# Sparse attention over 128 rows with zero-padded keys, dilated attention with its input in residue order

## The chip, the cores and the metric

One NeuronCore of a Trainium2 chip runs the whole program in one launch. The metric is device microseconds of that core. Five engines matter: TensorE (PE, with its weight loads shown apart as PEld), VectorE (DVE), ScalarE (ACT), GpSimd (POOL), and SyncE (SP), which issues the transfers. Every engine works through its own instructions in order.

## What is computed

The reference is two transformer blocks on 512 tokens of width 1024. The first mixes three branches (a gated linear recurrence, sparse attention, gated linear attention) and ends in a dense feed-forward. The second is a state-space mixer and a dilated-attention mixer, each followed by a mixture of 32 experts. The change touches the sparse attention of the first block and the dilated attention of the second.

```python
# sparse attention: 16 heads in 4 groups g of 4 heads r, head dim 64
kc = compress_blocks(k_cmp, ...)          # 31 compressed keys per group
o_cmp = softmax(q . kc + bias) . vc
sel   = top 8 of 8 blocks of 64 keys      # all blocks, 512 tokens
o_slc = softmax(q . k_slc + bias) . v_slc # causal
o_win = softmax(q . k_win + bias) . v_win # last 256 keys
o = g0 * o_cmp + g1 * o_slc + g2 * o_win
# dilated attention: groups (window, dilation) = (128,1), (512,4), (2048,16)
q, k = rope(x @ wq), rope(x @ wk);  v = x @ wv
o, m, l = attention of each residue class of tokens mod dilation
```

## The kernel before, in words

Large products are split into a high part in fp32r and a low remainder, three matmuls for each 128-deep slice: high x high, high x low, low x high. `piece2` loads 256 weight columns (1 MB) into one of the weight slots (`wslot` goes round a list, `self.order`, of five), ACT makes the high part `whi`, DVE and POOL the remainders. `g_fm2` (matmul on L351) then writes features by tokens with 512 token columns moving, two blocks of 128 features each of 24 matmuls; `g_tm2` (L368) writes tokens by features with 256 columns moving, four blocks of 24 matmuls.

**Sparse attention.** `cmp_keys` puts the keys and values to be compressed into `kt`, `cmp_hidden` multiplies them by `cmp_w1` (L659, plain fp32, 155 columns gathered from `kt` with a step of 16 elements), `cmp_out` forms the compressed keys `kcH`, `kcL` and values `vc`. For each group `nsa_q` makes the queries `Q`: 64 rows hold the high part and the other 64 rows the low part, so one 128-row matmul against the high keys, copied into both halves (`KH`, L827), adds both. The low keys `KL` have 64 rows that hold data; a second matmul (L828) takes only these 64 rows of `Q` and of `KL`. So 128-row and 64-row matmuls alternate:

```python
nc.tensor.matmul(w, lhsT=Q[:, i, qs], rhs=KH[:, ty, k0:k1], start=True, ...)
nc.tensor.matmul(w, lhsT=Q[H, i, qs], rhs=KL[H, ty, k0:k1], stop=True, ...)
```

`nsa_cmp` does the same with 32 compressed keys (L782 with `kcH`, L784 with `kcL`). `nsa_a` adds the bias and takes maximum, exponential and scale on DVE, ACT and POOL; `nsa_c` transposes the weights (L851, four heads a time), splits them (`ph` on ACT, `pl` on DVE) and multiplies with `V` (L855, L856). The compressed part of it has 32 rows: four transposes of 128x32, then two 512-column matmuls with 32 rows against `vc`.

`nsa` walks over 32 steps, one for a group, a block of 128 queries and a kind (selected, window). While step n is in its `nsa_c`, step n+1 is in its `nsa_a`, and units of projections that come later (`Fill`) are put between. The order on each engine is then made by the framework's planner.

**Dilated attention.** `att_begin` and `att_tile` transpose the layer-normed input, 128 tokens a time, in the tail of the first expert stage (`transpose_split`, L433 and L434), tokens in their natural order. `att_qk` projects queries and keys by `g_fm2`, turns them by rope, and POOL writes the sum in residue order: for the 16-fold and 4-fold groups at once, for the queries of group 0 in four pieces. `att_v` projects values of the groups 1 and 2 by `g_tm2` with every fourth token column of `xT` as the weights that are loaded (`tok=lambda v, t: v[:, t::4]`), so each block of 128 tokens is one residue class, and ACT copies it out. `att` then runs the three groups with `att_a` (scores L1758, softmax) and `att_c` (L1784 transposes, L1793 products), projections of the next group between them as fill: `att_v(2)` beside group 0, `att_v(1)` beside the first half of group 1.

Of the kernel before, what the change touches and what calls it, by code (L numbers as in the profile page):

```python
# [88 lines left out]
def make_consts():  # L89
# [16 lines left out]
    c.add("am0", np.where(np.concatenate([k >= tq, k <= tq], 1), 0.0, BIG))  # L106
# [44 lines left out]
class Base:  # L151
# [206 lines left out]
    def g_tm2(self, segs, x, evac, tok=lambda v, t: v[:, 128 * t:128 * t + 128]):  # L358
# [4 lines left out]
        for t in range(4):  # L363
            ps = self.mm("lin", "lin")
            for k in range(8):
                xh, xl = x(k)
                for i, (w, v) in enumerate(((hi, xh), (lo, xh), (hi, xl))):
                    nc.tensor.matmul(ps[:, :width], lhsT=tok(v, t), rhs=w[:, k, :width],  # L368
                                     start=(k == 0 and i == 0), stop=(k == 7 and i == 2))
                if self.fine and k == 3:  # L370
                    yield
# [52 lines left out]
    def transpose_split(self, src, hi, lo, t):  # L424
# [3 lines left out]
        for h in range(2):  # L428
# [4 lines left out]
            nc.scalar.activation(hi[:, 4 * h:4 * h + 4, c], v, AF.Copy)  # L433
            nc.vector.tensor_tensor(lo[:, 4 * h:4 * h + 4, c], v, hi[:, 4 * h:4 * h + 4, c], op=OP.subtract)  # L434


class Block1:
# [144 lines left out]
    def nsa_tables(self, st, q):  # L582
# [5 lines left out]
        self.vc = p.tile([32, 4, 128], R, name="vc")  # L588
# [33 lines left out]
    def cmp_setup(self, st):  # L622
        q = self.cq = self.pool(st, "cmp", side="right")

        self.ckt = [q.tile([128, 5, 512], F, name=f"kt{i}") for i in range(2)]
        pos = q.tile([32, 2, 64], F, name="pos")
        self.nc.sync.dma_start(pos, self.a["cmp_pos"][0].rearrange("y j d -> j y d"))
        for ty in range(2):
# [4 lines left out]
            pv = pp[:64, :32].rearrange("p (j e) -> p e j", e=2)  # L633
            for e in range(2):
                self.nc.vector.tensor_copy(t[64 * e:64 * e + 64, 4, 0:32:2], pv[:, e])

    def cmp_keys(self, x):

        nc = self.nc
        for ty in range(2):  # L640
            def ev(j, ps):
                t = self.ckt[ty]
                for h in range(2):
                    s = ps[64 * h:64 * h + 64]
                    nc.scalar.activation(t[0:64, 2 * j + h], s, AF.Copy)
                    nc.vector.tensor_copy(t[64:128, 2 * j + h, 0:511], s[:, 1:512])
# [3 lines left out]
    def cmp_hidden(self, ty):  # L650
# [5 lines left out]
        for m in range(2):  # L656
            ph = self.mm("ph", "lg")
            for j in range(16):
                nc.tensor.matmul(ph[:, 0:155], lhsT=w1[j // 8][:, j % 8, 128 * m:128 * m + 128],  # L659
                                 rhs=self.ckt[ty][:, :, 2 * j:2 * j + 481:16], start=(j == 0), stop=(j == 15))  # L660
# [16 lines left out]
    def cmp_out(self, ty):  # L677
# [3 lines left out]
        if ty == 0:  # L681
# [5 lines left out]
            nc.vector.tensor_copy(z[:, :, 0:31], pk[:64, :124].rearrange("p (g c) -> p g c", g=4))  # L687
            for e in range(2):
                r = slice(64 * e, 64 * e + 64)
                nc.scalar.activation(self.kcH[r], z, AF.Copy)  # L690
                nc.vector.tensor_tensor(self.kcL[r], z, self.kcH[0:64], op=OP.subtract)
        else:
# [11 lines left out]
            nc.scalar.activation(self.vc[:, :, 0:64], zh, AF.Copy)  # L704
            nc.vector.tensor_copy(self.vc[:, :, 64:128], zl)
# [17 lines left out]
    def nsa_kv(self, hf, x):  # L723
        nc, w_in, p = self.nc, self.a["w_in"][0], self.ngp
        o = hf * 128
        KL = p.tile([128, 2, 512], R, name="KL", bufs=2)
        for g in range(2):
            self.nK[2 * hf + g] = p.tile([128, 2, 512], R, name="KH", bufs=3), KL
            self.nV[2 * hf + g] = p.tile([128, 4, 2, 128], R, name="V", bufs=3)

        def ev_k(j, ps):
            for g in range(2):
                s = ps[64 * g:64 * g + 64]
                KH = self.nK[2 * hf + g][0]
# [38 lines left out]
    def nsa_cmp(self, g):  # L773
# [3 lines left out]
        H = slice(64 * (g % 2), 64 * (g % 2) + 64)  # L777
        pc = self.mm("pc", "lg")
        pcv = pc.rearrange("p (b h c) -> p b h c", b=4, h=4)
        for b in range(4):  # L780
            for h in range(4):
                nc.tensor.matmul(pcv[:, b, h], lhsT=Q[:, h, 128 * b:128 * b + 128], rhs=self.kcH[:, g],  # L782
                                 start=True, stop=False, skip_group_check=True)
                nc.tensor.matmul(pcv[:, b, h], lhsT=Q[H, h, 128 * b:128 * b + 128], rhs=self.kcL[H, g],  # L784
# [18 lines left out]
    def nsa_a(self, g, b, ty, out):  # L803
# [3 lines left out]
        H = slice(64 * (g % 2), 64 * (g % 2) + 64)  # L807
# [11 lines left out]
        for h in range(4):  # L819
            at = h % per * n  # L820
            if at == 0:
                ps = self.mm("lg", "lg")
                buf = sp.tile([128, 512], F, name="S", bufs=8)
                for i in range(h, h + per):
                    for c, k0, k1 in rng:
                        w = ps[:, (i - h) * n + c:(i - h) * n + c + k1 - k0]
                        nc.tensor.matmul(w, lhsT=Q[:, i, qs], rhs=KH[:, ty, k0:k1], start=True, stop=False, skip_group_check=True)  # L827
                        nc.tensor.matmul(w, lhsT=Q[H, i, qs], rhs=KL[H, ty, k0:k1], start=False, stop=True, skip_group_check=True)  # L828
# [17 lines left out]
    def nsa_pv(self, O, src, V, first, last, n=128):  # L846
# [3 lines left out]
        for h in range(4):  # L850
            nc.tensor.transpose(pt[:n, 128 * h:128 * h + 128], src(h), self.ident)  # L851
        ph = tp.tile([128, 512], R, name="ph")[:n]
        pl = tp.tile([128, 512], R, name="pl")[:n]
        self.split(pt[:n], ph, pl)
        nc.tensor.matmul(O, lhsT=V, rhs=ph, start=first, stop=False, skip_group_check=True)  # L855
        nc.tensor.matmul(O, lhsT=V, rhs=pl, start=False, stop=last, skip_group_check=True)  # L856

    def nsa_c(self, g, b, ty, A, C, yd):
# [11 lines left out]
        for i, (pos, kb) in enumerate(order):  # L870
            self.nsa_pv(O, lambda h: S[h][:, 128 * pos:128 * pos + 128], V[:, kb, ty], ty == 0 and i == 0, False)
# [1486 lines left out]
```

## Time and profile before

| | us |
|---|---|
| three runs | 3441.3, 3443.03, 3443.37 |
| median | 3443.03 |
| the profiled execution, its own time | 3444.63 |
| span of its profile (first to last instruction) | 3442.8 |
| PE busy | 3286.1 (95%) |
| DVE, ACT, POOL busy | 1474.6, 1008.2, 731.6 |

The span is cut into stretches by the program's order: setup and recurrence up to about 170 us, compression of keys and first projections up to about 280 us, sparse attention 280 to 632 us, then gated linear attention, merge, feed-forward, state-space mixer, the first experts (from about 1928 us), dilated attention 2516 to 2832 us, and the second experts up to the end. An engine counts as busy from the start of an instruction to its modelled end, so PE reads full even where its matmuls follow one another slowly; the distance between the starts of two matmuls tells how fast it goes.

### The profile page before, as it was taken

Reading aid. Unit: us, or ns where it says so; the run is one execution under the profiler, and the core shown is the slowest. Engines: PE = TensorE matmul, PEld = TensorE weight load, DVE = VectorE, ACT = ScalarE, POOL = GpSimd, SP = SyncE. Lnnn points to the kernel's source line nnn. Section 1 sums busy time; section 2 is a strip of 40 time slices with the busy share of each in tenths; the row PEclk is TensorE's granted clock in tenths of the full one; section 3 lists DMA queues with packets and bytes.
Section 4 is the critical chain, followed back from the end, with each engine's and each line's share of the span. In section 5 each row is a group of like instructions: output and inputs, shape, how many; then the busy total and the mean of one; then the engine's idle time right before and its main releaser. Section 6 shows DMA issues by size and latency. Waiting matters only on the chain. (4 is left out here: it accounts for less than half of the span.)

```text
span 3442.8 us, 40245 instructions
## 1 busy us (share of the span) xinstructions
PE 3286.1 (95%) x15295; PEld 2263.3 (66%) x15295; DVE 1474.6 (43%) x3023; ACT 1008.2 (29%) x1871; POOL 731.6 (21%) x567
## 2 busy tenths in 40 slices
PE   6899999999998999999999899999999988999997
PEld 5677777787886888877777544444489885444443
DVE  4835455632224323278777522222453445222223
ACT  3525444742233222244333201000233332000001
POOL 2422222432333222103333200000163412000000
PEclk9999897999998999999999899999999998999999
DMA  8231111123333233233332699999821225999996
GB/s 186 86 115 46 42 37 31 50 86 116 117 117 119 90 95 98 63 110 99 106 107 96 249 389 362 380 351 351 308 62 50 62 86 214 390 360 378 356 347 254
DMA packets 289986, 599.26 MB, mean 174 GB/s; under 512 B 29104, under 2 KB 150316, under 8 KB 289756
## 3 DMA queue, kind: packets, MB, share of 16 engines
q1 hardware_dynamic: 289788, 596.63, 50.0%
q8 instruction: 123, 2.02, 0.2%
q14 instruction: 75, 0.61, 0.1%
HBM read 584.94 MB, written 11.60 MB: 173 GB/s over the span
## 5 line engine op out<-in xcount | busy, mean ns | idle before, releaser
L332 POOL TENSOR_TENSOR lob<-rawb,whi 128x1024 fp32r<-128x1024 f32 (+1 forms) x53 | 137.0, 2586 | 791.0 <-ACTq L2156 538.4
L262 PE MATMUL mm<-hT,whi 128*128 128x512 f32 x960 | 300.0, 394 | 0.0
L351 PE MATMUL lin<-hT,whi 128*128 128x512 f32 (+1 forms) x784 | 268.5, 421 | 21.7 <-ACT gs L534 15.9
L2076 PE MATMUL mm<-rawb,XG 128*64 128x512 f32 x704 | 262.1, 600 | 0.0
L2076 PE MATMUL mm<-rawa,XG 128*64 128x512 f32 x704 | 258.4, 599 | 0.0
L242 DVE TENSOR_TENSOR loa<-rawa,whi 128x1024 fp32r<-128x1024 f32 (+2 forms) x94 | 116.8, 1243 | 298.4 <-ACT whi L241 297.0
L242 POOL TENSOR_TENSOR lob<-rawb,whi 128x1024 fp32r<-128x1024 f32 x56 | 141.7, 2530 | 438.8 <-ACT whi L241 395.9
L262 PEld LDWEIGHTS mm<-hT,whi 128*128 128x128 f32 x960 | 180.7, 188 | 44.1 <-ACT hT L433 0.2
L241 ACT ACTIVATE whi<-rawa 128x1024 fp32r<-128x1024 f32 (+2 forms) x94 | 94.6, 1006 | 357.6 <-issue 191.8
L351 PEld LDWEIGHTS lin<-hT,whi 128*128 128x128 f32 (+1 forms) x784 | 152.2, 197 | 65.5 <-ACT gs L534 16.8
L2211 PEld LDWEIGHTS xg<-OH,X 128*128 128x128 f32 x1024 | 133.3, 195 | 78.1 <-issue 74.6
L2139 PE MATMUL cmb<-yy,sel 128*128 128x512 f32 x512 | 156.3, 428 | 13.1 <-ACT yy L2119 3.6
L2139 PEld LDWEIGHTS cmb<-yy,sel 128*128 128x128 f32 x512 | 90.7, 192 | 112.4 <-issue 59.5
L2211 PE MATMUL xg<-OH,X 128*128 128x256 f32 x1024 | 153.5, 298 | 2.7 <-DVE OH L2201 2.7
L389 POOL TENSOR_TENSOR ln<-lnv,mhalf 128x1 f32<-128x1 f32 x16 | 13.4, 840 | 605.7 <-DVE lnv L387 602.1
L368 PE MATMUL lin<-whi,hT 128*128 128x256 f32 x640 | 130.1, 294 | 0.8 <-ACT gv L952 0.8
L262 PE MATMUL mm<-xT,whi 128*128 128x512 f32 (+1 forms) x400 | 129.5, 404 | 1.2 <-ACT xT L433 1.2
L2113 PE MATMUL py<-rawa,H 128*64 128x512 f32 x288 | 129.9, 598 | 0.0
L2076 PEld LDWEIGHTS mm<-rawa,XG 128*64 128x64 f32 x704 | 69.9, 136 | 89.9 <-issue 83.6
L2113 PE MATMUL py<-rawb,H 128*64 128x512 f32 x288 | 126.6, 598 | 0.0
L351 PE MATMUL lin<-xT,whi 128*128 128x512 f32 x384 | 123.5, 399 | 0.0
L2076 PE MATMUL mm<-mraw,XG 128*64 128x512 f32 x336 | 123.3, 602 | 0.0
(609 smaller groups left out, 7355.3 us busy)
## 6 DMA issues: line engine op xcount, KB each, us to landing
rawa<-in_moe_w_up_dram SPq DMA_DIRECT2D x92, 512.0 KB, 7.7
rawb<-in_moe_w_up_dram SPq DMA_DIRECT2D x92, 512.0 KB, 10.2
rawa<-in_moe_w_gate_dram SPq DMA_DIRECT2D x84, 512.0 KB, 10.2
rawb<-in_moe_w_gate_dram SPq DMA_DIRECT2D x84, 512.0 KB, 9.3
rawa<-in_moe_w_down_dram SPq DMA_DIRECT2D x72, 512.0 KB, 7.8
rawb<-in_moe_w_down_dram SPq DMA_DIRECT2D x72, 512.0 KB, 9.1
mrawp<-in_moe_w_down_dram SPq DMA_DIRECT2D x60, 512.0 KB, 10.2
mraw<-in_moe_w_gate_dram SPq DMA_DIRECT2D x52, 512.0 KB, 8.5
```

The source lines that it names most:

```text
L241: nc.scalar.activation(h, t[:, :, :o], AF.Copy)
L242: (self.second if j else nc.vector).tensor_tensor(lo[:, :, :o], t[:, :, :o], h, op=OP.subtract)
L262: nc.tensor.matmul(ps[j][:m], lhsT=w[:, k, 128 * j:128 * j + m], rhs=v, start=(kc + k == 0 and i == 0), stop=(kc + k == K - 1 and i == 2))
L332: (nc.gpsimd if j or self.late > 0 else nc.vector).tensor_tensor(lo, t, h, op=OP.subtract)
L351: nc.tensor.matmul(ps[:m], lhsT=w[:, k, 128 * j:128 * j + m], rhs=v, start=(k == 0 and i == 0), stop=(k == 7 and i == 2))
L368: nc.tensor.matmul(ps[:, :width], lhsT=tok(v, t), rhs=w[:, k, :width], start=(k == 0 and i == 0), stop=(k == 7 and i == 2))
L389: self.nc.gpsimd.tensor_tensor(r, v, self.half[:, :n], op=OP.pow)
L2076: nc.tensor.matmul(ps[64 * u:64 * u + 64], lhsT=XG(4 * h + k, u), rhs=w[u][k], start=(h == k == 0), stop=(h == 1 and k == 3), skip_group_c ...
L2113: nc.tensor.matmul(py[c][s], lhsT=H[:, 2 * h + k, s], rhs=w[u][2 * k + c], start=(h == k == 0), stop=(h == k == 1), skip_group_check=True, ...
L2139: nc.tensor.matmul(ps, lhsT=sel[rows, 128 * t:128 * t + 128], rhs=yy[rows, hl, s], start=(n == 0), stop=(n == 2 * len(group) - 1))
L2211: nc.tensor.matmul(s, lhsT=X2[t][:, hl, k], rhs=OH[:, t], start=(hl == t == 0), stop=(hl == 1 and t == 3))
```

## The change

In the sparse attention the low keys get 128 rows, of which the 64 without data are set to zero by POOL (DVE for `kcL`), and both matmuls of a pair take all 128 rows of `Q`. Each group has low keys of its own (`nKL`, three buffers; two lie in weight slot 4, so the weights go round four slots until the sparse attention ends). The compressed weights of the four heads are transposed together as 128x128, split as 128x128, and multiplied in eight 128-column matmuls with `vc` in 128 rows, of which 32 at a time are not zero (`nsa_pc`). `kt` is laid out so that the 155 columns of L659 are runs of 31 neighbours, and ACT and DVE each copy 256 of 512 columns into it.

In the dilated attention `transpose_split` writes each tile of 128 tokens in residue order (four residues of 32 tokens), the rope angles and the mask of group 0 follow, group 0 takes queries and keys as they come, and groups 1 and 2 write with runs of 32. `att_v` uses `g_fm2` with 512 token columns moving, copies the result out on ACT, transposes it back on PE (16 transposes a call) and copies it out again on DVE.

Lines of the diff without effect on the argument (an argument of `g_tm2` that goes, two unused variables) are left out.

```diff
@@ -103,7 +103,8 @@ make_consts
-    c.add("am0", np.where(np.concatenate([k >= tq, k <= tq], 1), 0.0, BIG))
+    tk = 4 * (k % 32) + k // 32
+    c.add("am0", np.where(np.concatenate([tk >= tq, tk <= tq], 1), 0.0, BIG))
...
@@ -430,8 +432,12 @@ transpose_split
-            nc.scalar.activation(hi[:, 4 * h:4 * h + 4, c], v, AF.Copy)
-            nc.vector.tensor_tensor(lo[:, 4 * h:4 * h + 4, c], v, hi[:, 4 * h:4 * h + 4, c], op=OP.subtract)
+            H, L = hi[:, 4 * h:4 * h + 4, c], lo[:, 4 * h:4 * h + 4, c]
+            if res:
+                v = v.rearrange("p k (j r) -> p k r j", r=4)
+                H, L = (w.rearrange("p k (r j) -> p k r j", r=4) for w in (H, L))
+            nc.scalar.activation(H, v, AF.Copy)
+            nc.vector.tensor_tensor(L, v, H, op=OP.subtract)
@@ -585,7 +591,9 @@ nsa_tables
-        self.vc = p.tile([32, 4, 128], R, name="vc")
+        self.vc = p.tile([128, 4, 4, 128], R, name="vc")
+        nc.gpsimd.memset(self.vc.bitcast(F), 0.0)
@@ -622,7 +630,7 @@ cmp_setup
-        self.ckt = [q.tile([128, 5, 512], F, name=f"kt{i}") for i in range(2)]
+        self.ckt = [q.tile([128, 5, 8, 32], F, name=f"kt{i}") for i in range(2)]
@@ -630,9 +638,9 @@ cmp_setup
-            pv = pp[:64, :32].rearrange("p (j e) -> p e j", e=2)
+            pv = pp[:64, :32].rearrange("p (c j e) -> p e j c", e=2, c=2)
-                self.nc.vector.tensor_copy(t[64 * e:64 * e + 64, 4, 0:32:2], pv[:, e])
+                self.nc.vector.tensor_copy(t[64 * e:64 * e + 64, 4, :, 0:2], pv[:, e])
@@ -642,8 +650,9 @@ cmp_keys
-                    nc.scalar.activation(t[0:64, 2 * j + h], s, AF.Copy)
-                    nc.vector.tensor_copy(t[64:128, 2 * j + h, 0:511], s[:, 1:512])
+                    v = s.rearrange("p (c j e) -> p e j c", e=2, j=8)
+                    nc.scalar.activation(t[0:64, 2 * j + h], v[:, 0], AF.Copy)
+                    nc.vector.tensor_copy(t[64:128, 2 * j + h], v[:, 1])
@@ -657,7 +666,7 @@ cmp_hidden
-                                 rhs=self.ckt[ty][:, :, 2 * j:2 * j + 481:16], start=(j == 0), stop=(j == 15))
+                                 rhs=self.ckt[ty][:, :, j % 8, j // 8:j // 8 + 31], start=(j == 0), stop=(j == 15))
@@ -685,10 +694,11 @@ cmp_out
+            nc.vector.memset(self.kcL.bitcast(F), 0.0)
-                nc.vector.tensor_tensor(self.kcL[r], z, self.kcH[0:64], op=OP.subtract)
+                nc.vector.tensor_tensor(self.kcL[r, e::2], z[:, e::2], self.kcH[0:64, e::2], op=OP.subtract)
@@ -701,8 +711,10 @@ cmp_out
-            nc.scalar.activation(self.vc[:, :, 0:64], zh, AF.Copy)
-            nc.vector.tensor_copy(self.vc[:, :, 64:128], zl)
+            for h in range(4):
+                r = slice(32 * h, 32 * h + 32)
+                nc.scalar.activation(self.vc[r, :, h, 0:64], zh, AF.Copy)
+                nc.vector.tensor_copy(self.vc[r, :, h, 64:128], zl)
@@ -723,15 +735,16 @@ nsa_kv
-        KL = p.tile([128, 2, 512], R, name="KL", bufs=2)
+            KL = self.nKL[(2 * hf + g) % 3]
+            nc.gpsimd.memset(KL[64 - 64 * g:128 - 64 * g].bitcast(F), 0.0)
-                KH = self.nK[2 * hf + g][0]
+                KH, KL = self.nK[2 * hf + g]
@@ -774,14 +787,13 @@ nsa_cmp
-        H = slice(64 * (g % 2), 64 * (g % 2) + 64)
-                nc.tensor.matmul(pcv[:, b, h], lhsT=Q[H, h, 128 * b:128 * b + 128], rhs=self.kcL[H, g],
+                nc.tensor.matmul(pcv[:, b, h], lhsT=Q[:, h, 128 * b:128 * b + 128], rhs=self.kcL[:, g],
...
@@ -825,7 +836,7 @@ nsa_a
-                        nc.tensor.matmul(w, lhsT=Q[H, i, qs], rhs=KL[H, ty, k0:k1], start=False, stop=True, skip_group_check=True)
+                        nc.tensor.matmul(w, lhsT=Q[:, i, qs], rhs=KL[:, ty, k0:k1], start=False, stop=True, skip_group_check=True)
@@ -843,17 +854,30 @@ nsa_pv, nsa_pc
-    def nsa_pv(self, O, src, V, first, last, n=128):
+    def nsa_pv(self, O, src, V, first):
         nc, tp = self.nc, self.ntp
         pt = self.tp()
         for h in range(4):
-            nc.tensor.transpose(pt[:n, 128 * h:128 * h + 128], src(h), self.ident)
-        ph = tp.tile([128, 512], R, name="ph")[:n]
-        pl = tp.tile([128, 512], R, name="pl")[:n]
-        self.split(pt[:n], ph, pl)
+            nc.tensor.transpose(pt[:, 128 * h:128 * h + 128], src(h), self.ident)
+        ph = tp.tile([128, 512], R, name="ph")
+        pl = tp.tile([128, 512], R, name="pl")
+        self.split(pt, ph, pl)
         nc.tensor.matmul(O, lhsT=V, rhs=ph, start=first, stop=False, skip_group_check=True)
-        nc.tensor.matmul(O, lhsT=V, rhs=pl, start=False, stop=last, skip_group_check=True)
+        nc.tensor.matmul(O, lhsT=V, rhs=pl, start=False, stop=False, skip_group_check=True)
+    def nsa_pc(self, O, C, g):
+        nc, tp = self.nc, self.ntp
+        pt = self.tp()
+        nc.tensor.transpose(pt[:, 0:128], C, self.ident)
+        ph = tp.tile([128, 512], R, name="ph")[:, 0:128]
+        pl = tp.tile([128, 512], R, name="pl")[:, 0:128]
+        self.split(pt[:, 0:128], ph, pl)
+        for h in range(4):
+            for i, v in enumerate((ph, pl)):
+                nc.tensor.matmul(O[:, 128 * h:128 * h + 128], lhsT=self.vc[:, g, h], rhs=v, start=False,
+                                 stop=(h == 3 and i == 1), skip_group_check=True)
@@ -868,11 +892,11 @@ nsa_c
-            self.nsa_pv(O, lambda h: S[h][:, 128 * pos:128 * pos + 128], V[:, kb, ty], ty == 0 and i == 0, False)
+            self.nsa_pv(O, lambda h: S[h][:, 128 * pos:128 * pos + 128], V[:, kb, ty], ty == 0 and i == 0)
-        self.nsa_pv(O, lambda h: C[:, b, h], self.vc[:, g], False, True, 32)
+        self.nsa_pc(O, C[:, b].rearrange("p h c -> p (h c)"), g)
@@ -1229,6 +1253,9 @@ block1
+                        self.order = range(4)
+                        self.nKL = [self.in_slot(f"KL{i}", 4, [128, 2, 512], R, 4096 * i) for i in range(2)]
+                        self.nKL.append(self.ngp.tile([128, 2, 512], R, name="KL"))
@@ -1254,6 +1281,7 @@ block1
+                    self.order = range(5)
@@ -1561,7 +1589,8 @@ rope_tables
-        nc.vector.tensor_copy(ang, pi)
+        nc.vector.tensor_copy(ang.rearrange("p (b r j) -> p b r j", b=4, r=4), pi.rearrange("p (b j r) -> p b r j", b=4, r=4))
@@ -1597,7 +1626,7 @@ att_tile
-        self.transpose_split(x[:, t], *self.xT, t)
+        self.transpose_split(x[:, t], *self.xT, t, True)
...
@@ -1717,26 +1745,30 @@ att_qk, att_v
-                    if perm == 0:
+                    if g == 0:
                         nc.gpsimd.tensor_tensor(d, s, r, op=OP.add)
-                    elif perm == 1:
-                        v = lambda t: t.rearrange("p (j r) -> p j r", r=4)
-                        nc.gpsimd.tensor_tensor(d.rearrange("p (r j) -> p j r", r=4), v(s), v(r), op=OP.add)
                     else:
-                        v = lambda t: t.rearrange("p (b j r) -> p b j r", b=4, r=4)
-                        for b in range(4):
-                            nc.gpsimd.tensor_tensor(d.rearrange("p (b r j) -> p b j r", b=4, r=4)[:, b],
-                                                    v(s)[:, b], v(r)[:, b], op=OP.add)
+                        v = lambda t: t.rearrange("p (b r j) -> p b r j", b=4, r=4)
+                        nc.gpsimd.tensor_tensor(d.rearrange("p (r b j) -> p b r j", b=4, r=4), v(s), v(r), op=OP.add)
                 yield from self.g_fm2([(w, 1536 * g + 512 * which + 256 * half, 256)], xx, ev)
     def att_v(self, g, w, xx):
+        nc = self.nc
         V = self.aT[g]["V"] = self.ap0.tile([128, 4, 512], F, name="V", tag="V")
         for half in range(2):
-            def ev(t, ps):
-                self.nc.scalar.activation(V[:, t, 256 * half:256 * half + 256], ps[:, :256], AF.Copy)
-            yield from self.g_tm2([(w, 1536 * g + 1024 + 256 * half, 256)], xx, ev, tok=lambda v, t: v[:, t::4])
+            def ev(j, ps):
+                s = self.ap2.tile([128, 512], F, name="rv", tag="rs")
+                nc.scalar.activation(s.rearrange("p (r b j) -> p b r j", b=4, r=4),
+                                     ps.rearrange("p (b r j) -> p b r j", b=4, r=4), AF.Copy)
+                pt = self.tp()
+                for r in range(4):
+                    nc.tensor.transpose(pt[:, 128 * r:128 * r + 128], s[:, 128 * r:128 * r + 128], self.ident)
+                c = 256 * half + 128 * j
+                nc.vector.tensor_copy(V[:, :, c:c + 128], pt.rearrange("p (r f) -> p r f", r=4))
+            yield from self.g_fm2([(w, 1536 * g + 1024 + 256 * half, 256)], xx, ev)
```

## Rows read from the trace of the kernel before

**Rows 1.** The page, busy time of each engine over the span.

```profile
PE 3286.1 (95%) x15295; PEld 2263.3 (66%) x15295; DVE 1474.6 (43%) x3023; ACT 1008.2 (29%) x1871; POOL 731.6 (21%) x567
```

**Rows 2.** Windows: stretch, length, busy time by engine, PE clock, DMA share, GB/s.

```profile
280.00:340.00 60.00, 59.67 (x289) 43.13 (x288) 41.00 (x155) 34.53 (x95) 18.07 (x21) 0.98 0.18 47
340.00:560.00 220.00, 219.56 (x1043) 168.77 (x1043) 113.81 (x379) 104.50 (x260) 51.44 (x57) 0.89 0.16 40
560.00:620.00 60.00, 59.37 (x192) 37.24 (x192) 38.25 (x138) 31.70 (x82) 13.99 (x17) 0.69 0.06 16
2516.00:2800.00 284.00, 284.00 (x1407) 248.22 (x1405) 110.15 (x329) 102.41 (x284) 113.35 (x83) 1.00 0.19 58
```

**Rows 3.** Instructions on tile Q: count, ns min/median/max, first and last start, forms.

```profile
L827 PEld LDWEIGHTS lg<-KH,Q x160: 186/187/337, 279.3 to 617.4; 128*128 128x128 f32 x160
L827 PE MATMUL lg<-KH,Q x160: 220/338/775, 279.3 to 617.4; 128*128 128x128 f32 x64, 128*128 128x256 f32 x64, 128*128 128x384 f32 x16, 128*128 128x512 f32 x16
L828 PE MATMUL lg<-KL,Q x160: 218/381/792, 279.5 to 617.7; 64*128 64x128 f32 x64, 64*128 64x256 f32 x64, 64*128 64x384 f32 x16, 64*128 64x512 f32 x16
...
L784 PE MATMUL pc<-kcL,Q x64: 228/392/393, 252.6 to 559.4; 64*128 64x32 f32 x64
```

**Rows 4.** Timeline of PE in the sparse attention: start, us, instruction, count.

```profile
341.71 0.39 PE L782 MATMUL pc<-kcH,Q 128*128 128x32 f32 x1
342.03 0.39 PE L784 MATMUL pc<-kcL,Q 64*128 64x32 f32 x1
...
469.37 0.32 PE L828 MATMUL lg<-KL,Q 64*128 64x128 f32 x1
469.62 0.33 PE L827 MATMUL lg<-KH,Q 128*128 128x128 f32 x1
...
472.18 0.39 PE L351 MATMUL lin<-hT,lob 128*128 128x512 f32 x1
472.41 0.28 PE L368 MATMUL lin<-whi,hT 128*128 128x256 f32 x1
472.52 0.28 PE L368 MATMUL lin<-loa,hT 128*128 128x256 f32 x1
...
475.51 0.38 PE L828 MATMUL lg<-KL,Q 64*128 64x256 f32 x1
475.82 0.38 PE L827 MATMUL lg<-KH,Q 128*128 128x256 f32 x1
...
548.05 0.28 PE L784 MATMUL pc<-kcL,Q 64*128 64x32 f32 x1
548.26 0.28 PE L782 MATMUL pc<-kcH,Q 128*128 128x32 f32 x1
```

**Rows 5.** Timeline of PE in the dilated attention.

```profile
2785.66 1.16 PE L1758 MATMUL sc<-kT,qT 64*128 64x128 f32 x8
...
2797.02 0.63 PE L368 MATMUL lin<-whi,xT 128*128 128x256 f32 x2
2797.49 0.40 PE L368 MATMUL lin<-lob,xT 128*128 128x256 f32 x1
```

**Rows 6.** Weight loads of line 368, from neighbouring and from every fourth column.

```profile
L368 PEld LDWEIGHTS lin<-whi,hT x640: 186/189/337, 274.5 to 751.0; 128*128 128x128 f32 x160
L368 PEld LDWEIGHTS lin<-whi,xT x256: 307/329/334, 2622.9 to 2799.0; 128*128 128x128 f32 x128
```

**Rows 7.** Timeline of PE, two plain fp32 products.

```profile
151.35 1.88 PE L512 MATMUL pg<-xc,lru_w 128*128 128x512 f32 x4
...
207.02 8.60 PE L659 MATMUL ph<-kt,raw 128*128 128x155 f32 x32
```

**Rows 8.** Instructions of lines 645 and 646, and who waited for 646.

```profile
L645 ACT ACTIVATE kt<-lin x8: 574/592/597, 172.2 to 193.6; 64x512 f32<-64x512 f32 x8
L646 DVE COPY kt<-lin x8: 682/688/694, 173.8 to 194.3; 64x511 f32<-64x511 f32 x8
...
  PE lin L351: 3.1, 2
```

More of the change, by code (lines that the diff above doesn't have):

```diff
@@ L356, in g_fm2, with g_tm2 @@
             yield
-    def g_tm2(self, segs, x, evac, tok=lambda v, t: v[:, 128 * t:128 * t + 128]):
+    def g_tm2(self, segs, x, evac):
         nc = self.nc
@@ L367, in g_tm2 @@
                 for i, (w, v) in enumerate(((hi, xh), (lo, xh), (hi, xl))):
-                    nc.tensor.matmul(ps[:, :width], lhsT=tok(v, t), rhs=w[:, k, :width],
+                    nc.tensor.matmul(ps[:, :width], lhsT=v[:, 128 * t:128 * t + 128], rhs=w[:, k, :width],
                                      start=(k == 0 and i == 0), stop=(k == 7 and i == 2))
@@ L422, in load_cols, with transpose_split @@
         return v
-    def transpose_split(self, src, hi, lo, t):
+    def transpose_split(self, src, hi, lo, t, res=False):
         nc = self.nc
@@ L806, in nsa_a @@
         Q, (KH, KL) = self.nQ[g], self.nK[g]
-        H = slice(64 * (g % 2), 64 * (g % 2) + 64)
         ns = 128 * (b + 1)
@@ L1709, in att_qk @@
             dst = self.aT[g][name] = self.ap1.tile([128, 4, 512], F, name=name, tag=name)
-            perm = 2 - 2 * which if g == 0 else 1
             for half in range(2):
```

## The prediction

> **What bounds the kernel now.** I read the page first: PE is busy 95% of the span and the next engine, DVE, 43% [rows 1]. That alone says little, because a PE instruction counts as busy to its modelled end. So I went to the windows of the two stages that the change touches. In the sparse attention PE is busy 338.6 of 340 us (59.67 + 219.56 + 59.37) and in the dilated attention 284 of 284, while DVE stands at 193.1 and ACT at 170.7 us of the 340, and DMA at 6 to 19% [rows 2]. Whatever shortens PE there shortens the kernel, until another engine or a chain of waits takes over. Last I read the timeline of PE, where the distance from one start to the next is the true price of a matmul. The reader is to see two things there. A 512-column product costs 0.23 us (472.18 to 472.41) and a 256-column one 0.11 to 0.12 (472.41 to 472.52). But where 128-row and 64-row matmuls alternate, 128 columns cost 0.25 (469.37 to 469.62), 256 columns 0.31 (475.51 to 475.82), and 32 columns 0.21 (548.05 to 548.26) or, where the clock was at half, 0.32 (341.71 to 342.03) [rows 4]. Eight 64-row matmuls in a row take 1.16 us together, 0.15 each [rows 5], so it is the change of height that costs, not the height. PE's clock is part of the picture: its mean is 0.98, 0.89 and 0.69 of full speed in the three stretches [rows 2]. With two levels, 2.4 and 1.2 GHz, that is 2 x 0.02 x 60 + 2 x 0.11 x 220 + 2 x 0.31 x 60 = 88 us at half speed.
>
> **Step 1, pairs of equal height.** The key products are 160 + 160 matmuls, of which 128 have 128 columns, 128 have 256, 32 have 384 and 32 have 512; the compressed ones are 64 + 64 of 32 columns [rows 3]. No row shows a 128-row fp32r product of 128 or 32 columns. From below it is what its columns take (0.06 for 128 by the 256-column step), from above the 256-column step; I take 0.12 for both, since the weight load of 128 columns comes with each and its latency is 187 ns whether 128 or 256 columns follow [rows 3, 4]. The gain for each is then 0.25 - 0.12 = 0.13 at 128 columns and 0.31 - 0.12 = 0.19 at 256; for 384 and 512 I take 0.20, one switch as at 256. Sum: 128 x 0.13 + 128 x 0.19 + 64 x 0.20 = 16.6 + 24.3 + 12.8 = 54 us. The compressed pairs lie about half at each clock: 128 x (0.265 - 0.12) = 19 us.
>
> Here a rule of the Trainium skill speaks against the change: its page "TensorE: Matmul & The Clock Gate" (Part 3, what overlaps and what doesn't) says that a weight load runs beside a matmul in flight only where their row groups differ. By that rule the pairs of 128 rows, which share all rows, would go no faster than now, and this step would give about 0 in place of 73 us. The trace disagrees for products of 128 rows on either side: loads of 189 ns in front of 256-column matmuls that start 0.11 to 0.12 us apart [rows 4, 6].
>
> **Step 2, the compressed values.** Four transposes and two 512-column products of 32 rows become one transpose and eight 128-column products, 1.1 us by the steps above. Before, they cost at least 2 x 0.23 + 4 x 0.11 = 0.9 us, and with one switch of 0.19 at each product 1.3. So 16 blocks lose or gain 3 us; I take 0. The copies shrink from 512 columns to 128, off the path.
>
> **Step 3, the clock.** Of the 88 us at half speed some 35 are the pairs of step 1. If half of the other 53 run at full speed, 53 x 0.5 x 0.5 = 13 us come back (bounds 0 and 26).
>
> **Step 4, what comes late next.** After steps 1 to 3 PE needs about 340 - 86 = 254 us for the stage, DVE still some 187 (193 less 16 short copies). That is 74%, above the 68% of its fullest stretch, 41.0 of 60 us [rows 2]. Where a step has no projection beside it, the chain scores, maximum, exponential, scale, transpose, split, product will show. At 68% the stage would take 187 / 0.68 = 275 us, 21 more; at 100% nothing. I take 9. Step 1 to 4 together: 54 + 19 + 0 + 13 - 9 = 77 us (bounds: 73 - 48 = 25 with the chain of rival A and no gain of clock; 73 + 3 + 26 = 102).
>
> **Step 5, compression of keys.** L659 takes 8.60 / 32 = 0.27 us for 155 columns with a step of 16 elements; the plain fp32 product of L512 with neighbouring columns takes 1.88 / 4 = 0.47 for 512, so 0.14 for 155 [rows 7]. With 128 of them in four such chains that is 128 x 0.13 = 16.6 us. The same factor of two shows on the weight side below, so I take it whole (bounds 0 and 17). Copies into `kt` halve, and PE waited 3.1 us for DVE's [rows 8]; I take 1.4 of it. Together 18 us.
>
> **Step 6, values of the dilated attention.** L368 with every fourth column costs 0.47 / 2 = 0.235 us (2797.02 to 2797.49) [rows 5], twice its price with neighbouring columns [rows 4]; the reason is the load, 329 ns against 189 [rows 6]. Two calls are 2 x 192 = 384 matmuls, 256 of them with `whi` [rows 6], so 384 x 0.235 = 90 us. After: 192 x 0.23 = 44, and 32 transposes at 0.12, 4 us. PE gains 42. The end of the last call is new: ACT copy, four transposes, DVE copy must pass before the first product with `V`; by rows of the same size 0.59 + 0.48 + 0.69 [rows 8], and I charge 2 us. Net 40 us. From below, PE could stand through the ACT copy before each of the eight groups of transposes, 8 x 0.59 = 5 us more: 35.
>
> **Edits at no cost.** Residue order in `transpose_split`, the rope angles, the mask and the writes of POOL keep the number of elements of each instruction; POOL has 113 of 284 us to do in that stage and loses four-piece sums [rows 2]. A strided read of 512 fp32 columns by ACT or DVE is not among my rows; if it were twice as long, 8 pairs of copies at 1.28 us [rows 8] in the tail of the first expert stage would cost at most 10 us. The zeroing of `KL` and `vc` is 5 instructions on POOL, which is busy 83.5 of 340 us [rows 2]; queued in front of a remainder `lob` each could hold a unit back by a few us, but a unit is asked for long before it is used. Four slots in place of five: behind a late transfer on SP stand the next weights and the stores of the results, and the stage moves 16 to 47 GB/s [rows 2], so three slots ahead are ample. Uncovered, each of the seven 1 MB pieces would wait 4 us for its transfer, if 47 GB/s at a share of 0.18 [rows 2] means 260 GB/s in full use.
>
> **Sum.** 77 + 18 + 40 = 135 us. The profiled execution took 3444.6 us, 1.6 above the median of the runs; 3444.6 - 135 = 3310, or 3308 as a median.
>
> **Rivals.**
> *A, the chain of the softmax sets the pace.* For it: DVE and ACT together are busy 364 of 340 us, and they take turns on each head [rows 2]. Against it: PE hardly idles today, 1.4 us in 340. If each of the 32 steps exposes 1.5 us, 48 us go in place of 9: 3347. The Trainium skill names this danger in "TensorEngine Tiling" (PSUM Bottleneck): copies out of PSUM do not get faster with TensorE. No row here shows that state yet.
> *B, equal heights do not help,* because the load of a full-width pair is exposed: 0.19 for the load [rows 3] plus 0.06 to 0.12 for the columns is 0.25 to 0.31, just today's steps. Then steps 1, 3 and 4 give nothing and 3385 is left. The 256-column steps of L368 speak against it [rows 4].
> *C, slower: the clock.* Between 560 and 620 us PE counted as busy and had a mean clock of 0.69 [rows 2]; 32-column matmuls in a dense row, or gaps behind DVE, could keep it at half speed. The stage's 267 us of work at full speed, less 26 for the clock, is about 241. It would need 340 + 58 = 398 us to eat the gain of steps 5 and 6, a mean clock of 0.6. At 0.55 the stage takes 438 us and the kernel 3483. The dilated attention, with a clock of 1.00 at the same density, speaks against it.
>
> **How the numbers follow.** The forecast (3275 to 3330) has a chance of 0.74, A (3330 to 3370) 0.16, B (3370 to 3400) 0.05, C 0.03, no change 0.02 if two of these meet. The bounds of the terms, 102 + 20 + 42 and 25 + 0 + 35, give 3279 and 3383; eight in ten lie between 3270 and 3350, which takes in most of A. A difference of 0.2% (7 us) is about what a measurement can tell from none. Faster 0.95, within it 0.02, slower 0.03.
>
> **What would show it.** In the changed kernel L827 and L828 should start 0.12 us apart at 128 and 256 columns; L659 should take 0.14; the values of the dilated attention should be 512-column products 0.23 apart. The sparse stage should last about 263 us, with PE waiting for DVE or ACT in steps without projections, and a mean clock of 0.95 or more. I am wrong if the pairs keep 0.25, if waits of PE in this stage add to over 40 us, or if the clock falls there.

## The result and the profile after

| | us |
|---|---|
| before, median of 4 runs (range) | 3442.16 (3434.36 to 3443.37) |
| after, median of 4 runs (range) | 3304.88 (3302.13 to 3308.55) |
| ratio (95% interval) | 0.9606 (0.9589 to 0.9624) |
| forecast | 3308 (3270 to 3350) |

The change takes 137 us off. Below, a part is bounded by starts of PE instructions: the sparse stage runs from the first key product to the last value product of the sparse attention, the dilated stage from the first product of `att_tile` to the last product with `V`.

| part of the profiled execution | before | after | difference |
|---|---|---|---|
| start to first key product | 279.3 | 257.1 | -22.1 |
| sparse stage | 353.4 | 280.2 | -73.2 |
| last value product to first experts | 1303.4 | 1298.3 | -5.1 |
| first experts to dilated stage | 545.6 | 544.9 | -0.7 |
| dilated stage | 342.9 | 304.0 | -39.0 |
| dilated stage to the end | 618.1 | 619.0 | +0.9 |

The 5.1 us behind the sparse stage go with 24 projection products that now lie inside it (below). The page of the changed kernel, engines over the span, answers [rows 1]; PE has 160 us less to do, DVE 16 more:

```profile
PE 3125.9 (95%) x15183; PEld 2161.4 (65%) x15183; DVE 1490.3 (45%) x3035; ACT 1000.7 (30%) x1866; POOL 736.5 (22%) x560
```

Its sparse stage in windows, with the columns of [rows 2], and below them the same stage of the kernel before as one window:

```profile
257.00:310.00 53.00, 47.67 (x300) 41.15 (x299) 42.27 (x147) 33.78 (x92) 20.67 (x20) 0.97 0.22 56
310.00:360.00 50.00, 46.54 (x303) 41.07 (x304) 41.31 (x143) 35.38 (x94) 16.99 (x22) 0.97 0.14 38
360.00:420.00 60.00, 59.95 (x375) 52.90 (x374) 39.07 (x115) 32.96 (x81) 17.27 (x17) 0.97 0.29 78
420.00:480.00 60.00, 59.48 (x430) 54.98 (x430) 42.10 (x137) 37.67 (x96) 21.28 (x23) 1.00 0.22 54
480.00:537.00 57.00, 47.48 (x239) 36.86 (x238) 44.27 (x150) 36.52 (x94) 18.17 (x22) 0.82 0.13 31
sum 280.00, PE 261.13 PEld 226.96 DVE 209.00 ACT 176.31 POOL 94.37; mean PE 52.23 PEld 45.39 DVE 41.80 ACT 35.26 POOL 18.87
...
279.00:632.00 353.00, 349.85 (x1569) 256.87 (x1567) 200.16 (x685) 178.16 (x450) 87.52 (x100) 0.86 0.14 37
```

Two things differ from before. The clock is near full speed except at the end, where there are no projections between the steps. And PE is idle for 18.9 of 280 us, in the first two windows and the last; before, it was 3.2 of 353.

The timeline of PE after, for the products of [rows 4] and [rows 7]:

```profile
207.81 5.69 PE L668 MATMUL ph<-kt,raw 128*128 128x155 f32 x42
213.24 0.50 PE L352 MATMUL lin<-hT,whi 128*128 128x512 f32 x1
...
316.06 0.26 PE L796 MATMUL pc<-kcL,Q 128*128 128x32 f32 x1
316.17 0.26 PE L794 MATMUL pc<-kcH,Q 128*128 128x32 f32 x1
...
435.21 0.29 PE L838 MATMUL lg<-KH,Q 128*128 128x256 f32 x1
435.33 0.28 PE L839 MATMUL lg<-KL,Q 128*128 128x256 f32 x1
435.45 0.22 PE L838 MATMUL lg<-KH,Q 128*128 128x128 f32 x1
435.51 0.27 PE L839 MATMUL lg<-KL,Q 128*128 128x128 f32 x1
435.62 0.33 PE L838 MATMUL lg<-KH,Q 128*128 128x256 f32 x1
```

From start to start, 256 columns cost 0.12 us, 128 columns 0.06 to 0.11, 32 columns 0.11, and the products of the compression 5.43 / 42 = 0.13. Each is about half of what it was, or less.

Where the 73 us of the sparse stage come from: the distances from each PE instruction to the next, added up by kind, with the part that fell into half clock.

| kind (instructions) | before, us | of it at half clock | after, us | of it at half clock |
|---|---|---|---|---|
| key products (320) | 100.2 | 23.3 | 55.1 | 6.1 |
| compressed keys (96 of the 128 lie in the stage) | 27.2 | 21.9 | 10.3 | 0.2 |
| compressed values (96; 144 after) | 22.6 | 8.0 | 17.5 | 2.2 |
| projections (600; 624 after), other values, transposes | 203.9 | 42.4 | 197.4 | 22.2 |

The time at half clock fell from 95.6 to 30.7 us in all. Set against the mean distance of each kind and size at full clock, that is worth some 27 of the 73 us, 15 of them in the two rows of the pairs.

### The profile page after: what moved, and what is told of

Read it like the earlier page. It is cut to its first block, busy times and chain, and to the rows that moved or that the text cites. A ratio compares the mean times of both kernels' runs of the same rounds, so it can differ in the third digit from the quotient of the medians.

```text
span 3303.5 us, 40014 instructions
## 1 busy us (share of the span) xinstructions
PE 3125.9 (95%) x15183; PEld 2161.4 (65%) x15183; DVE 1490.3 (45%) x3035; ACT 1000.7 (30%) x1866; POOL 736.5 (22%) x560
## 5 line engine op out<-in xcount | busy, mean ns | idle before, releaser
L352 PE MATMUL lin<-xT,whi 128*128 128x512 f32 x512 | 165.3, 400 | 0.0
```

Of the source, the lines that this page charges most:

```text
L352: nc.tensor.matmul(ps[:m], lhsT=w[:, k, 128 * j:128 * j + m], rhs=v, start=(k == 0 and i == 0), stop=(k == 7 and i == 2))
```

## Experiments

The first run takes the dilated half of the change alone; the second tests the reason for it.

**Dilated attention alone.** The kernel before with only the edits in `transpose_split`, the angles, the mask, `att_qk` and `att_v`.

> The kernel before with the dilated-attention part of the change alone. My theory: the stage from the first value product to the last product with V shortens by 40 us (90 us of 256-column products with every fourth column loaded become 44 us of 512-column ones, 4 us of transposes are added, 2 us of tail), so the ratio to before is 0.988 and the sparse attention keeps its 353 us. Rival: the two parts depend on each other (transfers or the planner's order), and alone this part gives less than 25 us.

3402.78 us, ratio 0.990 (0.9877 to 0.9922), so 34 us; its dilated stage took 304.9 in place of 342.9, so 38. The sparse stage, which this run leaves as it was, took 357.4 in place of 353.4, with 105.8 us at half clock. So the dilated part gives the same without the rest.

**The reason for it: the columns of the weights.** The kernel before, where `att_v` takes neighbouring columns. The values then come in natural order, which is not what the reference computes, so the stage alone is read.

```diff
-            yield from self.g_tm2([(w, ...)], xx, ev, tok=lambda v, t: v[:, t::4])
+            yield from self.g_tm2([(w, ...)], xx, ev)
```

> The kernel before with att_v loading 128 neighbouring token columns as weights instead of every fourth, so the values of groups 1 and 2 are in natural order and no longer the ones the reference needs; the routing of the second experts can change with them, so the stage alone is read. My theory (the step of four in the load is the price, not the 256 columns): 384 products fall from 0.235 to 0.12 us, and the stretch from the first value product to the last product with V falls from 343 to 296 to 303 us. Rival (256-column products with 128 tokens as weights are slow here for another reason): 343 us stays.

3391.03 us, ratio 0.9857 (0.9829 to 0.9884); the dilated stage took 299.0 us. The same 384 products took 47.5 us, before 91.6; the 192 products of 512 columns of the changed kernel take about 47. Their weight load (ns min/median/max, in the instructions of that line) answers to the 329 ns of [rows 6]:

```profile
L368 PEld LDWEIGHTS lin<-whi,xT x256: 186/189/196, 2620.8 to 2752.9; 128*128 128x128 f32 x128
```

**The low products back to 64 rows.** The changed kernel, where only the operands of the low products change.

```diff
-  lhsT=Q[:, i, qs], rhs=KL[:, ty, k0:k1]
+  lhsT=Q[H, i, qs], rhs=KL[H, ty, k0:k1]      # and kcL the same
```

> The changed kernel with one thing undone: the second product of each pair takes the 64 rows that hold data again (zeroing, buffers and everything else stay). My theory: 73 us of changes of height come back, and some of the half-speed clock with them, so 65 to 85 us slower than the changed kernel (ratio to before 0.980 to 0.985). Rival (after the change the chain through DVE and ACT sets the pace of the sparse attention, so PE's price there no longer counts in full): less than 40 us slower than the changed kernel.

3375.06 us, ratio 0.9826 (0.980 to 0.9851), 70 us more by the medians than with 128 rows, 73 by the spans. The stage took 345.2 us and 82 us of it were at half clock. Its pairs, on PE's timeline, cost what they had in [rows 4]:

```profile
420.67 0.36 PE L840 MATMUL lg<-KH,Q 128*128 128x256 f32 x1
420.97 0.38 PE L841 MATMUL lg<-KL,Q 64*128 64x256 f32 x1
421.28 0.33 PE L840 MATMUL lg<-KH,Q 128*128 128x128 f32 x1
421.54 0.33 PE L841 MATMUL lg<-KL,Q 64*128 64x128 f32 x1
```

**Is it 64 rows or the change of height?** The kernel before, all high products of a tile first and then all low ones, heights as they were.

```diff
-  for i in range(h, h + per):
-    for c, k0, k1 in rng:
-      matmul(w, Q[:, i, qs], KH[:, ty, k0:k1], start=True, stop=False)
-      matmul(w, Q[H, i, qs], KL[H, ty, k0:k1], start=False, stop=True)
+  for part in range(2):
+    for i in range(h, h + per):
+      for c, k0, k1 in rng:     # high if part == 0, else low
```

> The kernel before, still with 64-row low keys, but inside one PSUM tile all 128-row products are issued first and then all 64-row ones. My theory (a change of height costs 0.13 to 0.20 us, the height itself nothing): of 448 alternating products about 264 lose their change of height, so 36 to 50 us less than before (ratio 0.985 to 0.990), with 64-row products in a row about 0.12 to 0.15 us apart. Rival (a 64-row product is slow in itself, or the second product of a pair waits for the first since both add into the same columns): no change within 7 us.

3495.53 us, ratio 1.018, but the sparse stage took 309.5. Here every high product has `start=True`, and in this order the sums are no longer those of before: other tokens go to other experts (15575 PE instructions in place of 15295), and their first stage took 648.6 us in place of 545.6. The total says nothing. With the flag at the first high product of a tile alone, and nothing else changed, there are 15295 again:

> The kernel before with the products of one PSUM tile ordered by height (all 128-row ones, then all 64-row ones), only the first of them clearing the tile, so that the sums are those of before. My theory (a change of height costs 0.13 to 0.20 us): the sparse attention falls from 353 us to 305 to 317, and the kernel by 36 to 50 us against before (ratio 0.985 to 0.990). Rival (64 rows are slow in themselves, or a pair waits for its shared columns): no change within 7 us.

3389.6 us, ratio 0.9866 (0.9843 to 0.9889), the stage 309.0, the experts 545.6. On PE's timeline four of each height stand together:

```profile
409.54 0.56 PE L832 MATMUL lg<-KH,Q 128*128 128x128 f32 x4
410.02 0.66 PE L834 MATMUL lg<-KL,Q 64*128 64x128 f32 x4
410.61 1.96 PE L784 MATMUL pc<-kcH,Q 128*128 128x32 f32 x16
```

Four 64-row products of 128 columns cost 0.59 / 4 = 0.15 us each and four 128-row ones 0.48 / 4 = 0.12, each with the turn behind the last of them, against 0.25 in turns. Inside either group most starts lie 0.11 us apart, and the last product of a group costs 0.20. So half height is as fast here; the turn is the cost. Nor is it that the two products of a pair add into the same columns, one behind the other: in the changed kernel they still do.

**The layout of `kt`.** The changed kernel, with the 155 columns eight apart in place of neighbours.

```diff
-  t = q.tile([128, 5, 8, 32])    rhs = kt[:, :, j % 8, j // 8:j // 8 + 31]
+  t = q.tile([128, 5, 32, 8])    rhs = kt[:, :, j // 8:j // 8 + 31, j % 8]
```

> The changed kernel with the layout of kt turned so that neighbouring columns of the compression product L659 lie 8 elements apart instead of 1; copies keep their 256 columns. My theory: the moving operand is read at half the rate, L659 goes back from 0.13 to 0.26 us, 128 of them, 16 to 17 us slower than the changed kernel. Rival (the gain came from the halved copies into kt or from the order of the projections around it): no change within 4 us.

3323.93 us, ratio 0.9679 (0.9659 to 0.9699), 19 more. On PE's timeline each product costs 18.12 / 64 = 0.28 us:

```profile
205.54 18.12 PE L668 MATMUL ph<-kt,raw 128*128 128x155 f32 x64
```

**Compressed values as before.** The changed kernel with four transposes and two 512-column products of 32 rows.

> The changed kernel with the compressed values multiplied as before: four transposes of 128x32 and two 512-column products of 32 rows a block. By step 2 of the prediction: no change within 3 us. By the steps in the two traces (22.6 us for these instructions before, 17.5 after, and a change of height around them): 5 to 10 us slower than the changed kernel.

3318.58 us, ratio 0.9651 (0.9632 to 0.967), so 14 us by the medians, 6.5 by the spans (3310.0). The stage took 288.9, 8.7 longer; the compressed values 20.2 in it against 17.5, with 2.2 at half clock in either run. The stage also began 3 us sooner, and 19 more projection products fell into it.

**Is DVE the next limit?** Two DVE copies of 256 columns behind each of the 76 `split`s, in the kernel before and in the changed one.

> The kernel before with two copies more on DVE for each of the 76 blocks of value products in the sparse attention (256 columns each, into a scratch tile, read by nobody): 38 to 53 us of DVE work. My theory: PE sets the pace there, DVE is at 57%, so no more than 8 us slower than before. Rival (DVE's chain is on the path already): over 15 us slower.

> The changed kernel with the same added DVE copies. My theory: DVE is at 75% of the sparse attention and PE already waits for it, so 15 to 40 us slower than the changed kernel (3320 to 3345 against 3305). Rival (PE alone still sets the pace): no more than 8 us slower.

Before: 3438.78 us, ratio 1.0009 (0.9995 to 1.0024): 49.0 us of DVE, and no difference clear of noise; but the stage had 24 us less at half clock than in the kernel before, which may hide some of the cost. After: 3314.11, ratio 0.9644 (0.9621 to 0.9666): 9 us more by the medians for 53.9 of DVE, and 13 in the stage, of which 7 go with its time at half clock (44.4 us for 30.7). In this window of the changed kernel with the copies, DVE is busy 244 of 293 us:

```profile
256.00:549.00 293.00, 271.42 (x1637) 232.78 (x1636) 243.93 (x840) 177.11 (x456) 95.49 (x102) 0.92 0.19 50
```

A quarter or less comes through, under the 15 to 40 that I had expected. DVE delays some steps; it does not set the pace.

**What DVE is late with.** The waits of PE in the changed kernel's stage, largest first (us, times, longest):

```profile
PE O L867 <- DVE pl L216: 6.0, 10, 1.5
PE lg L838 <- DVE M L841: 5.3, 6, 1.2
PE O L866 <- ACT ph L215: 3.6, 2, 2.9
```

Before, the largest between 252 and 634 us was this:

```profile
PE O L855 <- ACT ph L214: 1.7, 2, 1.4
```

The instructions on tile `M` (ns min/median/max) show one that takes up to seven times its median before (L835) and fourteen times after (L846); below them its busy time in the stage (us, mean ns):

```profile
L835 DVE TENSOR_SCALAR M<-M x64: 106/160/1157, 283.1 to 619.3; 128x2 f32<-128x2 f32 x64
L846 DVE TENSOR_SCALAR M<-M x64: 106/163/2344, 262.9 to 521.5; 128x2 f32<-128x2 f32 x64
...
L835 DVE TENSOR_SCALAR M<-M 128x2 f32<-128x2 f32 x64 | 11.6, 191 | 0.3
L846 DVE TENSOR_SCALAR M<-M 128x2 f32<-128x2 f32 x64 | 23.8, 378 | 0.2
```

The timeline of DVE at its longest:

```profile
341.50 2.34 DVE L846 TENSOR_SCALAR M<-M 128x2 f32<-128x2 f32 x1
343.76 0.41 DVE L841 CUSTOM_DVE_ANT_0 S<-lg,nsa_ring 128x256 f32<-128x256 f32 x1
```

And that of POOL at the same time (start, length):

```profile
340.84 2.98 POOL L333 TENSOR_TENSOR lob<-rawb,whi 128x1024 fp32r<-128x1024 f32 x1 [7.41 <-ACT whi L332]
```

The two-column negation ends as POOL's remainder ends, at 343.8. To test it, the 64 negations go to ACT:

```diff
-  nc.vector.tensor_scalar(M[:, m], M[:, m], -1.0, None, op0=OP.mult)
+  nc.scalar.activation(M[:, m], M[:, m], AF.Copy, scale=-1.0)
```

> The changed kernel with the 64 negations of the row maxima (128x2) in the softmax done by ACT instead of DVE. In the changed kernel they take 23.8 us on DVE against 11.6 before, eight of them 1.1 to 2.3 us each, while a GpSimd instruction runs. My theory (they wait for GpSimd on the chain that PE now partly waits for, and a fifth of DVE's time comes through): 3 to 8 us faster than the changed kernel. Rival (ACT, at 63% of the stage, is as late as DVE): no change within 3 us, or slower.

3296.33 us, ratio 0.9588 (0.9571 to 0.9605). The intervals overlap, but its five runs (3294.9 to 3300.03) all lie below those of the changed kernel, by 8.5 us at the median and 8.6 in the span (6 by the ratios): a version that beats both. The stage took 272.9; PE's wait for `M` fell from 5.3 to 2.6 us, and its idle time from 18.9 to 12.9. DVE has 18 us less to do in the stage's window:

```profile
256.00:529.00 273.00, 260.05 (x1642) 226.62 (x1641) 190.91 (x625) 185.05 (x520) 94.22 (x102) 0.95 0.21 53
```

The instruction in its new place has no long cases (tile `M` of this run):

```profile
L846 ACT ACTIVATE M<-M x64: 187/203/208, 261.8 to 515.2; 128x2 f32<-128x2 f32 x64
```

**Four slots.** First the kernel before, whose weights go round four slots in this stage with nothing put into the fifth.

```diff
   self.nQ, self.nK, self.nV = {}, {}, {}
+  self.order = range(4)        # and range(5) again after nsa
```

> The kernel before with the weights going round four slots instead of five while the sparse attention lasts, nothing else. My theory (three transfers ahead are ample at 40 GB/s): no change within 4 us. Rival (the seven units wait for their transfers): 15 to 30 us slower than before.

3453.1 us, ratio 1.0045 (1.0025 to 1.0065): about 15 us, 7 by the spans (3450.1) and 10 in the stage. So fewer slots are not free. Of the 10, the sums show 9 in the projections (24 more of them, and 13 more us of them at half clock); PE's gaps grew from 3.2 to 7.6. Ahead of the stage PE waited once for a transfer that it does not wait for in the kernel before:

```profile
PE ph L659 <- DMA raw<-in_cmp_w_dram: 2.0, 1, 2.0
```

Then the other way, in the changed kernel with the compressed values of the run above, where a fifth slot has room again:

> The changed kernel with the compressed values as they were before (as in the run with the old compressed values), so that their tile is small again and all three tiles KL fit beside the five slots: the weights of the sparse attention go round five slots as before the change. The tile yt takes a turn of pl to make room. It is to be read against the run with the old compressed values, 3318.6 us, ratio 0.965, 288.9 us from the first key product to the last value product. Theory that four slots cost the changed kernel what they cost the kernel before (15 us, 10 of them in that stage): about 3304, ratio 0.961, stage about 279. Theory that four slots are ample in the changed kernel, as the prediction had it: 3315 to 3322, ratio 0.964 to 0.966, stage 286 to 292. If the turn that yt takes of pl costs more than the slot gives back, the stage is longer than 292.

3311.44 us, ratio 0.9635 (0.9617 to 0.9653), against 3318.58 and 0.9651 with four. The stage took 282.4 against 288.9, with 43 projections fewer in it, between what the two theories asked for (279, and 286 to 292); at the start of the dilated stage both stood at the same time, 2382.7 and 2383.2, and the spans are 3310.7 and 3310.0. In the changed kernel I can't tell the fifth slot from nothing.

## Why the prediction was right, step by step

**Step 1, pairs of equal height: the mechanism right, 73 forecast, the number in part by luck.** The key products fell by 45.1 us, and 5.9 more of what is left is gap in which PE waited, so 51 for 54. All 128 compressed products fell from 34.1 to 13.7, 20 for 19. That it is the turn, and not the height, is shown by the runs with the high products first and with 64 rows again. But not all of the 71 us is the turn. By the mean distances at full clock, without the gaps, the key products fell by 44 us where I had charged 54, and the compressed ones by 12.5 (0.10 each), which is what I had for them without the clock. Key products of 128 columns gained 0.14 us each for 0.13, those of 256 columns 0.14 for 0.19, the longer ones 0.12 to 0.14 for 0.20. The other 15 us are the clock inside the pairs, of which my sum had 7 (0.265 in place of 0.21): the one error made up for most of the other. Rival B falls with the rows at 435 us. The rule that I had weighed in the Trainium skill ("TensorE: Matmul & The Clock Gate", Part 3) would have left the pairs at 0.25 to 0.31; this trace disagrees, 0.06 to 0.12 with all rows shared.

**Step 2, compressed values: mis-sized, 0 forecast.** They fell by 5.1 us in place, and the run with the old ones is 6.5 to 14 us slower. I had counted the new eight products at 0.12 and the old ones with a turn of height at each, and held the two for equal. In the run with the old ones they take 20.2 us at the clock of the new kernel, so 2.7 of the 5.1 are the products; the rest is the clock, which I had left out: 8.0 us of the old 22.6 were at half speed, 2.2 of the new 17.5.

**Step 3, clock: right, 13 forecast.** I took 53 us at half speed outside the pairs and let half of them recover. The table has 42.4 + 8.0 = 50.4 before and 24.4 after, so 26 / 2 = 13 us. In the pairs of the stage another 38.9 us left half clock, which stands under step 1. Rival C needed a mean of 0.6; it is 0.95 over the stage and 0.82 in its last window.

**Step 4, what comes late next: mis-sized, 9 forecast.** PE's idle time in the stage grew from about 3 to 18.9 us, so by 16. Where I expected the waits (no projections beside the step) is where they are: 16.9 of the 18.9 us lie in stretches of over 6 us without a projection. DVE was busy 209 us, not 187. Of the difference 7 us are a slip: my sum took 340 of the stage's 353 us, in all of which DVE was busy 200. Another 12 were not in the sum: the two-column negations took 23.8 us after and 11.6 before, because some of them stand behind POOL; 7.3 us of the stage came back when they left DVE. Rival A had asked for 1.5 us at each of 32 steps, 48 in all; the 18.9 us of idle time, and the 9 us that 53.9 us more of DVE work cost, refute it.

**Step 5, compression of keys: right, 18 forecast.** The products went from 0.25 to 0.13 us, 32.6 to 16.6 in all, and putting the columns apart again costs 19. With the 3.5 us of the 32 compressed products that lie ahead of the stage, that is most of the 22.1 before the first key product.

**Step 6, values of the dilated attention: right, 40 forecast.** 39.0 measured, 38 alone. With neighbouring columns and no transposes the stage takes 299.0; the transposes, their copies and the waits cost 5 to 6, where I had 4 + 2.

**Edits at no cost: right for the strided copies, unsure for the slots.** The copies of `transpose_split` took 596 ns (ACT) and 684 (DVE) as before. The five zeroings took 5.6 us of POOL; no run leaves them out. That four slots are ample was argued from transfers alone; in the kernel before they cost 7 to 15 us. In the changed kernel it is between nothing and the 7 us by which the medians differ, whose intervals overlap. Why the kernel before suffered is not settled: the sums show projections drawn into the stage, more of them at half clock, 4 us more of gaps, and the one wait for a transfer, and no run separates these.

**The whole.** The sparse stage gave 73 us for 77, the compression 22 for 18, the dilated stage 39 for 40. That the sum came within 4 us of the forecast is better than its terms were: the turns came out 10 us smaller and the clock in the pairs 8 us larger than I had them, and steps 2 and 4 are off by 5 and 7 us in opposite directions.

## What to carry to other kernels

Read a matmul's price from start to start, beside neighbours of the same height and of the other: the turn cost up to 0.19 us in a row of pairs and 0.12 to 0.14 a product over the stage at full clock (0.10 at 32 columns), while the 64 added rows of zeros cost nothing that shows. Operands with their columns apart cost twice as much on TensorE here (weights with a step of 4 elements, moving columns with a step of 8 or 16), and a layout change in a copy that happens anyway was free. When PE gets faster, add up the other engines from their rows after, not before: DVE's small instructions got longer without being changed.

## What the runs showed of the hardware

The negation on DVE, of 128x2 elements, takes 160 ns at the median with POOL idle at its start. In 13 cases of 64 a POOL instruction was running then; the median of these was 1139 ns and the longest 2344. Before, it was 9 cases and 1157 at most. Twelve of the 13 took over 200 ns, and all twelve end 22 to 29 ns behind the end of POOL's instruction; the thirteenth, beside a zeroing, took 169. The Trainium skill says in "SBUF — State Buffer" (Who interferes with whom) that `tensor_scalar` on DVE can take the ports that DVE shares with GpSimd, and that of the two the second one then waits for the whole instruction of the first. The trace agrees: the negation at 341.5 us ends with POOL's remainder.

TensorE's granted clock stayed near full in the changed stage although PE had more gaps: 95.6 us of the 353 before were at 1.2 GHz and 30.7 of the 280 after. With the low products at 64 rows again it was 82 us, and with the heights sorted 44. In the four other runs with the old pairs it was 72 to 106, so the fall to 31 and 44 is more than one run differs from the next. The half clock lies where PE has pairs, transposes and value products alone: 84 of the 95.6 us before, and 24 of the 30.7 after, are in stretches of over 6 us without a projection. Half clock costs a pair in turns less than twice its time: a 64-row product of 128 columns takes 0.25 us at full clock and 0.41 at half, one of 32 columns 0.21 and 0.32, while in the changed kernel 128 columns take 0.105 and 0.21. Whether the clock rose because the turns went or because those stretches became shorter, no run separates.
